# Four K tiles of a projection's last two column blocks as seven products, spread among plain chunks

## The chip, the cores and the metric

One NeuronCore of one Trainium2 chip runs the whole program. The metric is device time in microseconds (us) from the start to the end of one execution. A core has TensorE (PE; its weight loads are PEld), VectorE (DVE), ScalarE (ACT), GpSimd (POOL) and SyncE (SP); SP, and partly POOL and ACT, issue the DMA transfers. Each engine works through its own instructions in order, and semaphores hold one until another's result is there.

## The reference

A trunk of two encoder layers on x, 256 positions by 2048 channels in float32: an attention and pooling mixer, a gated MLP (FFN), an mLSTM mixer, and a second FFN. The change lies in the last step of the mLSTM mixer:

```python
hn = hsum * lax.rsqrt(jnp.mean(hsum * hsum, axis=-1, keepdims=True) + NORM_EPS)
hn = hn * h_norm.astype(jnp.float32).reshape(MLSTM_HEADS, MLSTM_HEAD_DIM)
y = (hn.reshape(b, s, MLSTM_W) * o_gate).astype(h.dtype)
return y @ w_out
```

`y` is 256x2048, `w_out` 2048x2048, and the product is added to x. x then goes through an RMS norm into the second FFN.

## The kernel before

**Precision and chunks.** Each operand of a matrix product is kept as a high and a low part in a format that TensorE takes at full rate, and a product is three matmuls (high x high, high x low, low x high). Weights stream from DRAM as chunks of 128x1024 (512 KB). `Stream.load` issues the transfer of a chunk into a raw buffer `w` (seven of them) on SP's queue, and `Stream.split` makes its two parts in `hl` (five buffers): ScalarE's cast for the high part (L167), VectorE's subtraction for the low one (L168). TensorE's instructions stand in the order in which the Python code writes them. In this layer the other engines' are ordered by a scheduler, which works with a model of its own of how long things take, at build time; on the chip each engine then keeps that order.

**The output projection.** `out_proj` multiplies the mixer's result `mcat` (16 K tiles of 128 channels, each with both parts, in two tiles of eight) by `w_out` in four column blocks of 512. A chunk holds two K tiles of one column block, that is 12 matmuls of 128x512 (2 K tiles, 2 row halves, 3 terms). Blocks 0 and 1 are built side by side, first the K tiles 0 to 11, then 12 to 15, which are the last two heads and come late. Then follow block 2 and block 3, eight chunks each. A block has a PSUM tile of two banks, of which there are two (`mm`). `residual` (L543) adds a finished block to x, and `norm.add` squares it and sends it through transposes (`xt`, L347) into the normed, transposed and split activation `xx` of the layer after (ScalarE's high half at L359, VectorE's low half at L362). One `xt` holds two K tiles in one bank.

**The small PSUM banks.** `psp` has two pools of two banks each. The transposes take them by turns; a tile can also ask for a side.

**The work woven in.** `Weave` runs generators while the projection's matmuls are recorded: the last two heads' gates (`og`, reciprocals at L997, `hn` at L1001), their transposes (`htr`, L1006), and the norm blocks.

**Preparation for the layer after.** The FFN's products already use sums of weight quarters. Some are made ahead, under this layer: a step loads 1 MB into `gm` (L120), VectorE makes four sums there in place (L124 to L127), and SP stores them to DRAM (L129). There is one `gm`, so the next load waits for the store. Where these steps stand is set by numbers of chunks (`places`). Others are made by transfers that add, issued by POOL (L139, L143). An FFN also has one more raw buffer, in memory that this layer gives back.

**Seven products.** The last FFN's down projection has a helper for two row halves and two column blocks at once. With A and B cut in quarters, `into` forms the result from seven products instead of eight. It takes a pair of K tiles at a time, four sums of quarters of A (`pair_sums`: six sums on VectorE, a cast, a low half) and four sums of quarters of B (`Stream.sums`: kind "sum" needs one 128x512 addition before its split, "chain" two, "left" one). It accumulates in four small banks, b1 and b5 on side 1, b6 and b4 on side 0, and adds them to x with plus and minus in nine 128x512 VectorE additions; one product is kept by a ScalarE copy (`ca`). A chunk of such a unit feeds two products, six matmuls.

Of the kernel before, what the change touches and what calls it, by code (L numbers as in the profile page):

```python
# [9 lines left out]
F32 = mybir.dt.float32  # L10
F32R = mybir.dt.float32r
# [5 lines left out]
P = 128  # L17
D = 2048
S = 256
KT = D // P  # L20
# [12 lines left out]
FCH = [4, 8, 8, 8, 8, 8]  # L33
DORDER = (0, 1, 3, 2)
# [3 lines left out]
WARM = 5  # L38
ATT_PARTS = [[4 + h for h in range(8)], [0, 1, 2, 3], [4 + h for h in range(8, 12)]]
ML_PARTS = [list(range(12)), list(range(12, 16))]  # L40

NG = 4 * KT
NB = D // 512
# [22 lines left out]
class Stream:  # L66
# [182 lines left out]
def trunk(ctx: ExitStack, tc: tile.TileContext, gx, xT, xn, call, catt, cml, weights, make, out):  # L249
    nc = tc.nc  # L250
    v, a, g, pe = nc.vector, nc.scalar, nc.gpsimd, nc.tensor

    def pool(name, bufs, **kw):
        return ctx.enter_context(tc.tile_pool(name=name, bufs=bufs, **kw))
# [9 lines left out]
    mmp = pool("mm", 2, space=PSUM)  # L264
# [22 lines left out]
    wv = Weave()  # L287
# [7 lines left out]
    def mm(out_, lhsT, rhs, start, stop):  # L295
        pe.matmul(out_, lhsT, rhs, start=start, stop=stop, skip_group_check=True)  # L296
# [211 lines left out]
    def mov_group(act, name, width=512, before=None, after=None):  # L508

        ps = mmp.tile([P, 2, 512 if width > 256 else width], F32, tag="mm", name=name)  # L510
        per = CH * P // width
        hl = None
        for k in range(KT):
            if k % per == 0:
                before and before(k)
                hl = st.next()
                after and after(k)
            src = act(k)
            c = (k % per) * width
# [20 lines left out]
    def residual(ps, b, eng=None):  # L540
        for t in range(2):
            xs = x[:, t, b * 512 : b * 512 + 512]
            v.tensor_add(xs, xs, ps[:, t])  # L543

    def out_proj(cat, norm, name, parts, ready):

        pss = [mmp.tile([P, 2, 512], F32, tag="mm", name=f"op{name}_{i}") for i in range(2)]
        for i, kts in enumerate(parts):
            ready(i)
            for ps in pss:  # L550
                mov_part(ps, cat, kts, i == 0, i == len(parts) - 1)
        for b in range(NB):
            if b >= 2:
                ps = mmp.tile([P, 2, 512], F32, tag="mm", name=f"op{name}_{b}")
                mov_part(ps, cat, sum(parts, []), True, True)
            else:
                ps = pss[b]
            residual(ps, b)
            norm.add(b)


    def attention_layer(norm, nxt):
        with ExitStack() as es:
            def lp(name, bufs):
                return es.enter_context(tc.tile_pool(name=name, bufs=bufs, reuse_waits="tile"))

            kp, tp, t1p = lp("att_c", 1), lp("att_t", 2), lp("att_1", 1)
            catb = []
# [154 lines left out]
            vt = kp.tile([P, 2, 2, 512], F32R, tag="vt", name="vt")  # L723
# [76 lines left out]
            ps = mov_group(xx, "kproj", 512, ahead, tables)  # L800
# [27 lines left out]
            def ready(i):  # L828
                wv.until(lambda: need[i] <= done)

            out_proj(cat, nxt, "0", ATT_PARTS, ready)


    def mlstm_layer(norm, nxt):
        with ExitStack() as es:
# [181 lines left out]
            for hp in range(MH // 2):  # L1017
                vf = t1p.tile([P, 2, 512], F32, tag="vf", name=f"mvf{hp}")
                for c, n in ((0, MD + 32), (MD, MD)) if hp == 0 else ((0, 512),):
                    ps = mov_group(xx, f"mv{hp}_{c}", n)  # L1020
# [19 lines left out]
            def ready(i):  # L1040
                wv.until(lambda: set(range(6 + 2 * i)) <= done)

            out_proj(cat, nxt, "1", ML_PARTS, ready)


    def ffn_layer(layer, norm, nxt):
# [259 lines left out]
def _mov(w):  # L1306

    return w.reshape(-1, 2, P, 512).transpose(0, 2, 1, 3).reshape(-1, P, CH * P)


def _out_chunks(w, parts):
    t = w.reshape(KT, P, D)

    def some(kts, c):
        return _mov(t[kts][:, :, c : c + 512].reshape(len(kts) * P, 512))

    out = [some(kts, c) for kts in parts for c in (0, 512)]
    return np.concatenate(out + [some(sum(parts, []), c) for c in range(1024, D, 512)])


def _half_chunks(t):

    t = t.reshape(-1, 2, P, 2, 512).transpose(0, 1, 3, 2, 4)[list(DORDER)]
    b11, b12, b21, b22 = (t[:, k, n] for k in range(2) for n in range(2))
    return (np.concatenate([b11, b12, b22, b21], axis=2), np.concatenate([b21[0::2], b21[1::2]], axis=2))


def _att_chunks(w_in, w_out):
    pool_w, q_w = 512, HEADS * HD
    cols = [pool_w + q_w, pool_w, pool_w + q_w + 512, pool_w + 512, pool_w + 1024]  # L1330
    a = [_mov(w_in[:, c : c + 512]) for c in cols]
    a += [_stat(w_in[:, c : c + 256], range(KT)) for c in (0, 256)]
    return np.concatenate(a), _out_chunks(w_out, ATT_PARTS)


def _ml_chunks(w_in, w_out):
    a = []
    for hp in range(MH // 2):
        c = 2 * D + hp * 512
        a.append(_mov(w_in[:, c : c + 512]) if hp else _stat(w_in[:, c + MD : c + 512], range(KT)))  # L1340
        for h in (2 * hp, 2 * hp + 1):
            for part in (0, 1):
                c = part * D + h * MD
                a.append(_stat(w_in[:, c : c + 256], range(KT)))
        wo = w_in[:, 3 * D + hp * 512 : 3 * D + hp * 512 + 512]
        a.append(_mov(wo))
    return np.concatenate(a), _out_chunks(w_out, ML_PARTS)


def _up_chunks(w):  # L1350
# [241 lines left out]
```

## Time and profile before

| what | us |
|---|---|
| median of 3 runs | 2149.03 |
| the profiled execution, its own time | 2149.48 |
| its span, first to last instruction | 2147.7 |
| TensorE busy in the span | 2141.4 |
| VectorE busy | 1808.7 |
| ScalarE busy | 1342.4 |

The profile is of one execution. Its span is 1.8 us shorter than its time, which includes what lies around the instructions. Busy time of TensorE counts pipelined matmuls, so that a matmul of 128x512 shows 390 ns though the next starts sooner. The projection of the mLSTM layer begins at 1353 us in the span and ends at 1446.

### The profile page before, as it was taken

Reading aid. Unit: us, or ns where it says so; the run is one execution under the profiler, and the core shown is the slowest. Engines: PE = TensorE matmul, PEld = TensorE weight load, DVE = VectorE, ACT = ScalarE, POOL = GpSimd, SP = SyncE. Lnnn points to the kernel's source line nnn. Section 1 sums busy time; section 2 is a strip of 40 time slices with the busy share of each in tenths; the row PEclk is TensorE's granted clock in tenths of the full one; section 3 lists DMA queues with packets and bytes.
Section 4 is the critical chain, followed back from the end, with each engine's and each line's share of the span. In section 5 each row is a group of like instructions: output and inputs, shape, how many; then the busy total and the mean of one; then the engine's idle time right before and its main releaser. Section 6 shows DMA issues by size and latency. Waiting matters only on the chain.

```text
span 2147.7 us, 31090 instructions
## 1 busy us (share of the span) xinstructions
PE 2141.4 (100%) x10740; PEld 1811.7 (84%) x10740; DVE 1808.7 (84%) x2553; ACT 1342.4 (63%) x1883; POOL 256.6 (12%) x320
## 2 busy tenths in 40 slices
PE   9999999999999999999999999999999999999999
PEld 7888888888888888889888888888888888888887
DVE  7686698989889798877888887779898888988998
ACT  7665566766567576656445554456675776766865
POOL 0222111111111111100000011101111111101000
PEclk9999999999999999999999999999999999999999
DMA  9989899999999999968898899988999999999985
GB/s 356 241 239 253 256 250 357 305 338 329 301 329 313 333 319 365 322 181 272 348 340 330 334 304 331 311 292 243 337 322 325 337 316 339 351 333 341 332 283 167
DMA packets 217520, 659.08 MB, mean 307 GB/s; under 512 B 27178, under 2 KB 29522, under 8 KB 210578
## 3 DMA queue, kind: packets, MB, share of 16 engines
q1 hardware_dynamic: 183280, 598.02, 76.8%
q0 software_dynamic: 31008, 55.33, 16.6%
q10 hardware_dynamic: 3074, 3.75, 0.7%
q8 instruction: 84, 1.38, 0.2%
q14 instruction: 74, 0.61, 0.1%
HBM read 627.58 MB, written 139.50 MB: 357 GB/s over the span
## 4 chain that ended last, share of the span: by engine, by line
PE 96%; DVE 2%; DMA 1%; issue 1%; ACT 0%; ACTq 0%; DVEq 0%; SPq 0%
PE dn L296 21%; PE p L296 21%; PE up L296 20%; PE op L296 6%; PE mk L296 4%; PE mq L296 4%; PE mo L296 4%; PE mv L296 4%; PE qproj L296 3%; PE kproj L296 1%; PE pool L296 1%; PE vproj L296 1%; PE tr L1183 1%; DVE hl L168 1%; PE h_dn L296 1%
## 5 line engine op out<-in xcount | busy, mean ns | idle before, releaser
L167 ACT CAST hl<-w 128x1024 fp32r<-128x1024 f32 (+2 forms) x921 | 954.3, 1048 | 584.4 <-PE dn L296 95.2
L168 DVE TENSOR_TENSOR hl<-w,hl 128x1024 fp32r<-128x1024 f32 (+1 forms) x922 | 1110.2, 1218 | 247.6 <-ACT hl L167 239.5
L296 PE MATMUL dn<-hl,g 128*128 128x512 f32 x1968 | 470.0, 391 | 0.0
L296 PE MATMUL up<-xx,hl 128*128 128x512 f32 (+1 forms) x2560 | 466.5, 337 | 0.0
L296 PEld LDWEIGHTS up<-xx,hl 128*128 128x128 f32 x2560 | 405.0, 188 | 63.7
L296 PEld LDWEIGHTS dn<-hl,g 128*128 128x128 f32 x1968 | 367.3, 188 | 75.4
L296 PE MATMUL p<-hl,sx 128*128 128x512 f32 x1152 | 304.2, 390 | 0.2 <-DVE hl L168 0.2
L296 PEld LDWEIGHTS p<-hl,sx 128*128 128x128 f32 x1152 | 212.2, 188 | 42.1 <-DVE hl L168 0.6
L296 PE MATMUL p<-hl,xx 128*128 128x512 f32 x864 | 236.3, 391 | 0.0
L139 POOL DMA_DIRECT2D G<-in_q x140 | 116.5, 838 | 653.0 <-DMA G<-in_q 625.3
L296 PEld LDWEIGHTS p<-hl,xx 128*128 128x128 f32 x864 | 158.2, 188 | 30.1
L143 POOL DMA_DIRECT2D G<-G x124 | 108.3, 874 | 555.9 <-DMA G<-in_q 218.6
L296 PE MATMUL mv<-hl,xx 128*128 128x512 f32 (+2 forms) x480 | 92.4, 350 | 0.0
L296 PE MATMUL mq<-xx,hl 128*128 128x512 f32 (+1 forms) x512 | 91.9, 337 | 0.0
L296 PE MATMUL mk<-xx,hl 128*128 128x512 f32 (+1 forms) x512 | 91.8, 338 | 0.0
L296 PE MATMUL op<-hl,cat 128*128 128x512 f32 x384 | 91.6, 393 | 0.0
L296 PE MATMUL mo<-hl,xx 128*128 128x512 f32 x384 | 90.4, 391 | 0.0
L296 PE MATMUL op<-hl,mcat 128*128 128x512 f32 x384 | 90.0, 392 | 0.3 <-DVE x L543 0.3
L296 PEld LDWEIGHTS mq<-xx,hl 128*128 128x128 f32 x512 | 79.2, 188 | 11.6
L296 PEld LDWEIGHTS mk<-xx,hl 128*128 128x128 f32 x512 | 78.8, 188 | 11.4
L296 PEld LDWEIGHTS mv<-hl,xx 128*128 128x128 f32 x480 | 78.1, 189 | 11.1
L296 PEld LDWEIGHTS op<-hl,mcat 128*128 128x128 f32 x384 | 71.3, 188 | 15.3 <-issue 0.7
(274 smaller groups left out, 2006.1 us busy)
## 6 DMA issues: line engine op xcount, KB each, us to landing
w<-in_dn SPq DMA_DIRECT2D x168, 512.0 KB, 7.6
w<-in_up SPq DMA_DIRECT2D x160, 512.0 KB, 8.0
w<-in_m_in SPq DMA_DIRECT2D x124, 512.0 KB, 6.4
w<-G SPq DMA_DIRECT2D x88, 512.0 KB, 8.4
w<-in_q SPq DMA_DIRECT2D x80, 512.0 KB, 8.5
G<-in_q SPq DMA_DIRECT2D x124, 256.0 KB, 7.7
G<-G POOLq DMA_DIRECT2D x124, 256.0 KB, 7.6
w<-in_q SPq DMA_DIRECT2D x120, 256.0 KB, 7.2
```

What stands on the lines that cost most here:

```text
L139: pin(add.dma_start(G[r, 0:512], src[r, 512:1024], accum_op=ALU.add))
L143: pin(add.dma_start(G[:, at : at + 512], G[:, of : of + 512], accum_op=ALU.add))
L167: (self.nc.vector.tensor_copy if i + c == 0 else self.nc.scalar.copy)(hl[:, 0, c : c + n], w[:, c : c + n])
L168: self.nc.vector.tensor_sub(hl[:, 1, c : c + n], w[:, c : c + n], hl[:, 0, c : c + n].bitcast(F32))
L296: pe.matmul(out_, lhsT, rhs, start=start, stop=stop, skip_group_check=True)
L1183: pe.transpose(tr[:, j, t * P : t * P + P], src[:, c : c + P], ident)
```

## The change

Blocks 0 and 1 stay as they were. In blocks 2 and 3 the K tiles 0 to 3 no longer go in plain chunks. They are one unit of seven products over both blocks: two pairs of K tiles, 7 chunks. Blocks 2 and 3 keep 6 plain chunks each, so the projection has 35 chunks where it had 32. After two plain chunks of block 2 the unit's chunks alternate with plain ones (four of block 2, two of block 3). The sums of A are made once the last heads are done (`cat_sums`), in tiles that the heads used; the kept product is `cam`. The weights are reordered on the host, outside the timed program. The numbers in `places` are moved by the three new chunks.

```diff
+ATT_HALF, ML_HALF = [], [0, 1, 2, 3]
...
+    def out_proj(cat, norm, name, parts, ready, tiles, half=None):
...
-        for b in range(NB):
-            if b >= 2:
-                ps = mmp.tile([P, 2, 512], F32, tag="mm", name=f"op{name}_{b}")
-                mov_part(ps, cat, sum(parts, []), True, True)
-            else:
-                ps = pss[b]
-            residual(ps, b)
+        for b in range(2):
+            residual(pss[b], b)
             norm.add(b)
+        rest = [k for k in sum(parts, []) if k not in tiles]
+
+        def block(b):
+            ps = mmp.tile([P, 2, 512], F32, tag="mm", name=f"op{name}_{b}")
+            for k in range(0, len(rest), 2):
+                last = k == len(rest) - 2
+                mov_part(ps, cat, rest[k : k + 2], k == 0, last)
+                if last:
+                    residual(ps, b)
+                yield
+
+        third, fourth = block(2), block(3)
+        if tiles:
+            next(third), next(third)
+            two, sum_of, room, sums_done = half
+            wv.until(lambda: norm.blocks == 2 and sums_done())
+            order = [(p, i) for p in range(len(tiles) // 2) for i in range(2)]
+            unit = into(2, two, sum_of, len(tiles) // 2, f"op{name}", order, room)
+            for _ in range(len(rest) // 2 - 2):
+                next(unit), next(third)
+            for _ in range(2):
+                next(unit), next(fourth)
+            next(unit)
+        for _ in third:
+            pass
+        norm.add(2)
+        for _ in fourth:
+            pass
+        norm.add(3)
...
+            def cat_sums():
+                sx.append(t1p.tile([P, 4, 2, 2, P], F32R, tag="vt", name="sxm"))
+                for p in range(2):
+                    tv = t1p.tile([P, 2, S], F32, tag="G", name=f"cs1{p}")
+                    raw = t1p.tile([P, 4, P], F32, tag="Amat", name=f"cr1{p}")
+                    pair_sums(two(p), tv, raw, [(slice(0, 4), sx[0][:, :, p, 0], sx[0][:, :, p, 1])])
+                    yield 3.5
+                sx.append(None)
...
-    at = len(weights) + len(ml)
+    at = len(weights) + len(ml) - 3
...
-    here = [(at + 8 + 14 * k, 5) for k in range(16)]
+    here = [(at + 11 + 14 * k, 5) for k in range(16)]
```

**Where instructions move.** VectorE ahead of the seventh head's last product `hn6`, whose transposes TensorE takes inside the projection. Before (`hl` are low halves of splits, `rv` and `re` the head's norm, `og` the gate, `gm` the prepared sums):

```order
L168 TENSOR_TENSOR hl538_12674<-w538_12598,hl538_12674 128x1024
L168 TENSOR_TENSOR hl539_12727<-w539_12619,hl539_12727 128x1024
L301 TENSOR_SCALAR rv_h7_12700<-hss7_12696 128x2
L168 TENSOR_TENSOR hl540_12745<-w540_12647,hl540_12745 128x1024
L305 TENSOR_TENSOR re_h7_12704<-ry_h7_12702 128x2
L306 TENSOR_TENSOR re_h7_12704<-re_h7_12704,rv_h7_12700 128x2
L307 TENSOR_SCALAR re_h7_12704<-re_h7_12704 128x2
L308 TENSOR_TENSOR re_h7_12704<-re_h7_12704,ry_h7_12702 128x2
L997 RECIPROCAL og6_12658<-og6_12658 128x256
L124 TENSOR_TENSOR gm_9031<-gm_9031 128x512
L168 TENSOR_TENSOR hl541_12762<-w541_12669,hl541_12762 128x1024
L1001 TENSOR_TENSOR hn6_12447<-hn6_12447,og6_12658 128x512
```

And now (`cs` and `cr` are the pair sums, `sxm` their low half):

```order
L169 TENSOR_TENSOR hl541_12762<-w541_12669,hl541_12762 128x1024
L451 SCALAR_TENSOR_TENSOR cr11_12981<-cr11_12981,cs11_12980 128x128
L452 TENSOR_TENSOR cr11_12981<-cr11_12981,cs11_12980 128x128
L307 TENSOR_TENSOR re_h7_12704<-re_h7_12704,rv_h7_12700 128x2
L453 TENSOR_TENSOR cr11_12981<-cr11_12981,cs11_12980 128x128
L308 TENSOR_SCALAR re_h7_12704<-re_h7_12704 128x2
L309 TENSOR_TENSOR re_h7_12704<-re_h7_12704,ry_h7_12702 128x2
L1022 RECIPROCAL og6_12658<-og6_12658 128x256
L125 TENSOR_TENSOR gm_9031<-gm_9031 128x512
L169 TENSOR_TENSOR hl542_12779<-w542_12718,hl542_12779 128x1024
L456 TENSOR_TENSOR sxm_12945<-cr11_12981,sxm_12945 128x4x128
L1026 TENSOR_TENSOR hn6_12447<-hn6_12447,og6_12658 128x512
```

Between the gate's reciprocals and `hn6` the pair sums have come in, and one split more (`hl542`). Ten rows of pair sums stand further ahead in the same stretch and are not shown.

TensorE at the start of block 2, before (`op1_2` is block 2, `xt3` the transposes of norm blocks 0 and 1):

```order
L347 MATMUL xt3_0_13055<-cst_87,x_90 128x128 x4
L296 MATMUL op1_2_13018<-hl551_12971,mcat0_10166 128x512 x6
L347 MATMUL xt3_2_13070<-cst_87,x_90 128x128 x4
L296 MATMUL op1_2_13018<-hl552_12991,mcat0_10166 128x512 x6
L347 MATMUL xt3_4_13090<-cst_87,x_90 128x128 x4
L296 MATMUL op1_2_13018<-hl552_12991,mcat0_10166 128x512 x6
L347 MATMUL xt3_6_13105<-cst_87,x_90 128x128 x4
L296 MATMUL op1_2_13018<-hl553_13029,mcat0_10166 128x512 x12
L296 MATMUL op1_2_13018<-hl554_13046,mcat1_11908 128x512 x12
```

And now (`h1`, `h5`, `h6`, `h4` are the unit's banks b1, b5, b6, b4):

```order
L348 MATMUL xt3_0_13079<-cst_87,x_90 128x128 x4
L297 MATMUL op1_2_13040<-hl551_12992,mcat0_10166 128x512 x6
L348 MATMUL xt3_2_13094<-cst_87,x_90 128x128 x4
L348 MATMUL xt3_4_13103<-cst_87,x_90 128x128 x4
L348 MATMUL xt3_6_13112<-cst_87,x_90 128x128 x4
L297 MATMUL h1_op1_13127<-hl552_13013,mcat0_10166 128x512 x3
L297 MATMUL h5_op1_13128<-hl552_13013,sxm_12945 128x512 x3
L297 MATMUL op1_2_13040<-hl553_13051,mcat1_11908 128x512 x12
L297 MATMUL h6_op1_13164<-hl554_13070,sxm_12945 128x512 x3
L297 MATMUL h4_op1_13165<-hl554_13070,mcat0_10166 128x512 x3
L297 MATMUL op1_2_13040<-hl555_13123,mcat1_11908 128x512 x12
```

The last two transposes follow the second directly, and right behind the fourth the unit starts, which takes all four small banks.

VectorE at the same place, before (`xx` from `xt3_6` are the low halves of K tiles 6 and 7):

```order
L168 TENSOR_TENSOR hl556_13117<-w556_13019,hl556_13117 128x1024
L362 SCALAR_TENSOR_TENSOR xx3_9018<-xt3_2_13070,gcol_88,xx3_9018 128x256
L362 SCALAR_TENSOR_TENSOR xx3_9018<-xt3_4_13090,gcol_88,xx3_9018 128x256
L362 SCALAR_TENSOR_TENSOR xx3_9018<-xt3_2_13070,gcol_88,xx3_9018 128x256
L124 TENSOR_TENSOR gm_9031<-gm_9031 128x512
L362 SCALAR_TENSOR_TENSOR xx3_9018<-xt3_4_13090,gcol_88,xx3_9018 128x256
L125 TENSOR_TENSOR gm_9031<-gm_9031 128x512
L168 TENSOR_TENSOR hl557_13138<-w557_13044,hl557_13138 128x1024
L362 SCALAR_TENSOR_TENSOR xx3_9018<-xt3_6_13105,gcol_88,xx3_9018 128x256
L126 TENSOR_TENSOR gm_9031<-gm_9031 128x512
L168 TENSOR_TENSOR hl558_13155<-w558_13079,hl558_13155 128x1024
```

And now:

```order
L169 TENSOR_TENSOR hl556_13138<-w556_13041,hl556_13138 128x1024
L363 SCALAR_TENSOR_TENSOR xx3_9018<-xt3_6_13112,gcol_88,xx3_9018 128x256
L363 SCALAR_TENSOR_TENSOR xx3_9018<-xt3_0_13079,gcol_88,xx3_9018 128x256
L363 SCALAR_TENSOR_TENSOR xx3_9018<-xt3_2_13094,gcol_88,xx3_9018 128x256
L363 SCALAR_TENSOR_TENSOR xx3_9018<-xt3_4_13103,gcol_88,xx3_9018 128x256
L125 TENSOR_TENSOR gm_9031<-gm_9031 128x512
L363 SCALAR_TENSOR_TENSOR xx3_9018<-xt3_6_13112,gcol_88,xx3_9018 128x256
L126 TENSOR_TENSOR gm_9031<-gm_9031 128x512
L127 TENSOR_TENSOR gm_9031<-gm_9031 128x512
L128 TENSOR_TENSOR gm_9031<-gm_9031 128x512
L169 TENSOR_TENSOR hl557_13159<-w557_13068,hl557_13159 128x1024
```

The low halves and the four sums of `gm` have moved ahead of the split `hl557`, which before stood behind the second sum. The second low half from `xt3_6` stands behind the first sum of `gm` in both.

More of the change, by code (lines that the diff above doesn't have):

```diff
@@ L543, in residual @@
             v.tensor_add(xs, xs, ps[:, t])
-    def out_proj(cat, norm, name, parts, ready):
+    def out_proj(cat, norm, name, parts, ready, tiles, half=None):
         pss = [mmp.tile([P, 2, 512], F32, tag="mm", name=f"op{name}_{i}") for i in range(2)]
@@ L829, in ready @@
                 wv.until(lambda: need[i] <= done)
-            out_proj(cat, nxt, "0", ATT_PARTS, ready)
+            out_proj(cat, nxt, "0", ATT_PARTS, ready, ATT_HALF)
     def mlstm_layer(norm, nxt):
@@ L1041, in ready, with two, ready_sums @@
                 wv.until(lambda: set(range(6 + 2 * i)) <= done)
-            out_proj(cat, nxt, "1", ML_PARTS, ready)
+            sx = []
+            def two(p):
+                return catb[0][:, 2 * p : 2 * p + 2]
+            def cat_sums():
[6 more added lines that the diff above has]
+                sx.append(None)
+            def ready_sums(i):
+                ready(i)
+                if i == 1:
+                    wv.add(cat_sums())
+            half = (two, lambda j, p: [sx[0][:, j, p, i, :] for i in range(2)],
+                    lambda: t1p.tile([P, 512], F32, tag="og", name="cam"), lambda: len(sx) > 1)
+            out_proj(cat, nxt, "1", ML_PARTS, ready_sums, ML_HALF, half)
     def ffn_layer(layer, norm, nxt):
@@ L1308, in _mov, with _out_chunks @@
     return w.reshape(-1, 2, P, 512).transpose(0, 2, 1, 3).reshape(-1, P, CH * P)
-def _out_chunks(w, parts):
+def _out_chunks(w, parts, tiles):
     t = w.reshape(KT, P, D)
@@ L1317, in _out_chunks, with _out_order, _half_chunks @@
     out = [some(kts, c) for kts in parts for c in (0, 512)]
-    return np.concatenate(out + [some(sum(parts, []), c) for c in range(1024, D, 512)])
-def _half_chunks(t):
-    t = t.reshape(-1, 2, P, 2, 512).transpose(0, 1, 3, 2, 4)[list(DORDER)]
+    rest = [k for k in sum(parts, []) if k not in tiles]
+    out = {"out": np.concatenate(out + [some(rest, c) for c in range(1024, D, 512)])}
+    if tiles:
+        w = t[tiles][:, :, 1024:].reshape(len(tiles) * P, 1024)
+        out["four"], out["last"] = _half_chunks(w, range(len(tiles) // 2))
+    return out
+def _out_order(out, four=(), last=()):
+    if not four:
+        return out
+    n = (len(out) - KT) // 2
+    third, fourth = out[KT : KT + n], out[KT + n :]
+    unit = [(kind, q[:, c : c + 1024]) for q in four for kind, c in (("sum", 0), ("chain", 1024))]
+    unit += last + [("left", q[:, 512:1536]) for q in four]
+    plain = third[2:] + fourth[:2] + [None]
+    both = [e for pair in zip(unit, plain, strict=True) for e in pair]
+    return out[:KT] + third[:2] + both[:-1] + fourth[2:]
+def _half_chunks(t, order):
+    t = t.reshape(-1, 2, P, 2, 512).transpose(0, 1, 3, 2, 4)[list(order)]
     b11, b12, b21, b22 = (t[:, k, n] for k in range(2) for n in range(2))
@@ L1332, in _att_chunks @@
     a += [_stat(w_in[:, c : c + 256], range(KT)) for c in (0, 256)]
-    return np.concatenate(a), _out_chunks(w_out, ATT_PARTS)
+    return np.concatenate(a), _out_chunks(w_out, ATT_PARTS, ATT_HALF)
 def _ml_chunks(w_in, w_out):
@@ L1346, in _ml_chunks @@
         a.append(_mov(wo))
-    return np.concatenate(a), _out_chunks(w_out, ML_PARTS)
+    return np.concatenate(a), _out_chunks(w_out, ML_PARTS, ML_HALF)
 def _up_chunks(w):
@@ L1545 @@
         "call": call, "catt": catt, "cml": cml, "m_g": m_g,
-        "a_in": a_in, "a_out": a_out, "m_in": m_in, "m_out": m_out,
+        "a_in": a_in, "m_in": m_in, **{f"a_{k}": e for k, e in a_out.items()}, **{f"m_{k}": e for k, e in m_out.items()},
     }
@@ L1551 @@
         if HALF[l]:
-            arrays[f"hq{l}"], arrays[f"hb{l}"] = _half_chunks(i["w_down"][l][sum(FCH[:-1]) * P :, :1024])
+            arrays[f"hq{l}"], arrays[f"hb{l}"] = _half_chunks(i["w_down"][l][sum(FCH[:-1]) * P :, :1024], DORDER)
         arrays[f"q{l}"], arrays[f"b{l}"] = _quad_chunks(i["w_up"][l], UNITS[l])
@@ L1569 @@
     pairs = [_pairs(l, t[f"q{l}"]) for l in range(2)]
-    att, ml = chunks("a_in") + chunks("a_out"), vg + chunks("m_in") + chunks("m_out")
+    a_out, m_out = (_out_order(**{k: chunks(f"{n}_{k}") for k in e}) for n, e in (("a", a_out), ("m", m_out)))
+    att, ml = chunks("a_in") + a_out, vg + chunks("m_in") + m_out
     weights = att + ffn(0)
@@ L1581 @@
     pairs[1] += [(f"1h_{p}", 1, t["hq1"][p]) for p in range(4)]
-    places[1] += [(at + 246 + 14 * k, 6) for k in range(4)]
+    places[1] += [(at + 249 + 14 * k, 6) for k in range(4)]
     make = {}
```

## The prediction

> **What bounds the kernel now.** I read the page first, then TensorE's waits, then the stages of the projection, then its instructions engine by engine. The page's busy part and the largest groups, TensorE's waits, and four stages of the projection (busy us and instruction count for PE, PEld, DVE, ACT, POOL, then clock, DMA share, GB/s):
>
> ```profile
> span 2147.7 us, 31090 instructions
> PE 2141.4 (100%) x10740; PEld 1811.7 (84%) x10740; DVE 1808.7 (84%) x2553; ACT 1342.4 (63%) x1883; POOL 256.6 (12%) x320
> PE 96%; DVE 2%; DMA 1%; issue 1%; ACT 0%; ACTq 0%; DVEq 0%; SPq 0%
> ...
> L296 PE MATMUL op<-hl,mcat 128*128 128x512 f32 x384 | 90.0, 392 | 0.3 <-DVE x L543 0.3
> ```
>
> ```profile
> PE wps L320 <- DVE pad L762: 1.2, 1, 1.2
> PE htr L1006 <- DVE hn L1001: 0.3, 1, 0.3
> PE op L296 <- DVE x L543: 0.3, 1, 0.3
> ```
>
> ```profile
> 1353.00:1375.00 22.00, 22.00 (x106) 18.39 (x105) 20.13 (x26) 11.49 (x18) 3.15 (x4) 1.00 0.94 284
> 1375.00:1400.00 25.00, 24.70 (x111) 20.18 (x110) 13.99 (x18) 9.76 (x13) 2.44 (x3) 1.00 0.97 314
> 1400.00:1420.00 20.00, 20.00 (x97) 16.51 (x97) 13.88 (x20) 12.28 (x22) 2.59 (x4) 1.00 1.00 349
> 1420.00:1446.00 26.00, 26.00 (x120) 21.51 (x119) 16.42 (x19) 13.75 (x19) 1.52 (x2) 1.00 0.78 250
> ```
>
> TensorE is the chain, and its longest wait after the start is 0.3 us. So every matmul removed is a gain in full, and every wait added is a loss in full. Behind it VectorE has 64.4 of 93 us in the projection, 91% of the first stage. What decides the change is where VectorE and the transfers stand in order, not their sums.
>
> **The matmuls removed.** TensorE's part of the chain (start, us, what):
>
> ```profile
> 1399.76 4.37 PE op L296 x18
> ...
> 1409.62 0.44 PE xt L347 x4
> 1410.05 17.74 PE op L296 x78
> 1427.79 0.44 PE xt L347 x4
> ```
>
> 78 matmuls in 17.74 us: 0.227 us each, a plain chunk of 12 is 2.73 us, a unit's chunk of 6 is 1.36. Four K tiles in two column blocks are 48 matmuls; 2 pairs x 7 products x 3 are 42. Six fewer: **-1.4 us**.
>
> **Work added at nothing, if only totals counted.** Three chunks more (1.57 MB, 4.5 us at 349 GB/s, under the last stage's 22% of idle transfer time); three casts, two of the sums and one copy on ScalarE, some 5 us beside 47 busy of 93. VectorE gets three splits, eight weight additions, two pair-sum sets and nine additions into x and the kept product: about 18 us at the durations below, beside 64 busy of 93. The moved preparation numbers (+11, +249) keep their distance to the layer after. If the totals were the whole story the answer would be -1.4.
>
> **First place: the head's transpose.** VectorE in order (start, us, idle before it), and the transpose on TensorE:
>
> ```profile
> 1328.95 0.69 DVE L534 TENSOR_TENSOR tb_k<-mk,tb_k 128x512 f32<-128x512 f32 x1 [0.31 <-ACT tb_k L533]
> ...
> 1341.34 0.69 DVE L124 TENSOR_TENSOR gm<-gm 128x512 f32<-128x512 f32 x1 [1.04 <-DMA gm<-in_q]
> ...
> 1351.41 1.23 DVE L168 TENSOR_TENSOR hl<-w,hl 128x1024 fp32r<-128x1024 f32 x1 [1.41 <-ACT hl L167]
> ...
> 1354.82 0.77 DVE L995 TENSOR_SCALAR og<-og 128x512 f32<-128x512 f32 x2 [1.38 <-ACT og L991]
> ...
> 1361.52 1.23 DVE L168 TENSOR_TENSOR hl<-w,hl 128x1024 fp32r<-128x1024 f32 x1 [0.39 <-ACT hl L167]
> ...
> 1366.67 0.69 DVE L1001 TENSOR_TENSOR hn<-hn,og 128x512 f32<-128x512 f32 x1
> ...
> 1372.49 0.63 DVE L127 TENSOR_TENSOR gm<-gm 128x512 f32<-128x512 f32 x1
> ```
>
> ```profile
> 1369.76 0.60 PE L1006 MATMUL htr<-cst,hn 128*128 128x128 f32 x4
> ```
>
> hn ends at 1367.4 and is wanted at 1369.8: 2.4 us of slack. Ahead of it now stand ten 128x128 sums, a 128x512 sum, two low halves, one split and one sum of gm. The pair sums of the last layer price them, and splits and additions follow each other closer than their durations, as the x3 and the x2 show (a 128x128 sum by the same measure some 0.21):
>
> ```profile
> L448 DVE TENSOR_TENSOR cr<-cs x4: 283/288/293, 2041.4 to 2116.2; 128x128 f32<-128x128 f32 x4
> L455 DVE TENSOR_TENSOR sx<-cr,sx x4: 683/686/692, 2054.9 to 2121.8; 128x512 fp32r<-128x512 f32 x4
> ```
>
> ```profile
> 1420.89 3.49 DVE L168 TENSOR_TENSOR hl<-w,hl 128x1024 fp32r<-128x1024 f32 x3
> 1424.29 1.28 DVE L543 TENSOR_TENSOR x<-x,op 128x512 f32<-128x512 f32 x2
> ```
>
> That is 10 x 0.21 + 4 x 0.60 + 1.14 = 5.6 us. The gm set of 1341.34, for which VectorE waits 1.0 already, comes 1.6 us late as well: among the sums whose store it follows now stand the pair's first sum and tb_k, two of 0.6, with the 0.31 of wait. The three idle stretches shown absorb at most 3.2. hn is late by 5.6 + 1.6 - 3.2 = 4.0, less 2.4 of slack: **+1.6 us** (bounds: 0 if the idle stretches of other rows absorb it, 2.5 if only two of the three do). The last sum of that gm set then ends near 1378.0, not 1373.1: hn at 1371.3 and behind it 6.7 us of rows (three sums, hn of the second head, two splits, a reciprocal of 1.64, an mcat of 0.4).
>
> **Second place: the start of block 2.** VectorE and the two gm sets behind it:
>
> ```profile
> 1392.39 0.69 DVE L124 TENSOR_TENSOR gm<-gm 128x512 f32<-128x512 f32 x1 [5.92 <-DMA gm<-in_q]
> ...
> 1396.59 0.69 DVE L127 TENSOR_TENSOR gm<-gm 128x512 f32<-128x512 f32 x1
> ...
> 1398.34 1.28 DVE L543 TENSOR_TENSOR x<-x,op 128x512 f32<-128x512 f32 x2
> ...
> 1410.11 0.87 DVE L362 SCALAR_TENSOR_TENSOR xx<-xt,gcol,xx 128x256 fp32r<-128x256 f32 x2
> ...
> 1415.03 0.69 DVE L124 TENSOR_TENSOR gm<-gm 128x512 f32<-128x512 f32 x1 [3.41 <-DMA gm<-in_q]
> ```
>
> ```profile
> 1394.11 1.05 ACT L167 CAST hl<-w 128x1024 fp32r<-128x1024 f32 x1 [1.67 <-PE op L296]
> ```
>
> A gm set waits for the store of the last (L129) and a load (L120); each took, from issue to landing (min/median/max):
>
> ```profile
> DMA to landing us min/median/max: 5.6/8.1/11.2
> ```
>
> ```profile
> DMA to landing us min/median/max: 5.4/8.3/10.3
> ```
>
> From the end of one set to the next is so 16.4 us by the medians; the two above took 19.3 (from 1373.1) and 17.8 (from 1397.3). Taking 16.4 (the queues are no fuller than there), the set comes at 1378.0 + 16.4 = 1394.4, two sums, a split whose cast (the row on ScalarE) waits for TensorE and so ends 1.6 later, at 1396.8, a weight sum, a sum and the two additions: x is done at 1400.3. Blocks 0 and 1 end on TensorE at 1399.76 - 0.3, and 1.6 later now: 1401.1. So the 0.3 us wait there goes: **-0.3**. With 19.3 it is 0.9 of wait instead.
>
> **Third place: the unit's first chunk.** This is the term that decides. Its products take four PSUM banks at once (side 1 for b1 and b5), and the four transposes of norm blocks 0 and 1 have just filled the same four. b1 needs the bank of K tiles 2 and 3, b5 that of tiles 6 and 7, so both wait until VectorE has read the last low half from it. Before, nobody wanted these banks until the next transposes, at 1427.79. In the new order VectorE reaches tile 7's low half after the first sum of the next gm set, and that waits for its load.
>
> TensorE would be at b5 at 1401.1 + 2 x 2.73 + 4 x 0.44 + 0.68 = 1409.0. VectorE: the gm set ends at 1400.9, plus 16.4 is 1417.3, one sum 0.60, one low half 0.48: 1418.4. Wait: **+9.4 us**, in two pieces around the three products of b1.
>
> Bounds: even with the gm load there at once, VectorE has 17.8 us of rows from 1394.4 to that low half (five gm sums, six splits, four weight sums, four additions, eight low halves at 0.4) and stops for ScalarE's casts, which stand behind squares: 1414.8 at the earliest, a wait of 5.8. With the two durations seen it is 1421.3, against TensorE at 1410.0: 11.3, and 0.9 at the start of block 2.
>
> After that the splits of the next four chunks are done, and TensorE needs 8.9 us for them; the split behind (L168) ends 3 us after the release. No further wait of weight until the FFN by this count.
>
> **Sum**: -1.4 + 1.6 - 0.3 + 9.4 = +9.3, on the profiled execution's own 2149.48: 2158.8. The median of the runs, 2149.03, stands 0.45 lower, so **2158.4 us**. Its own range by the bounds of the third place (an earlier or later hn only shifts time between the waits): -1.4 + 1.6 - 0.3 + 5.8 = +5.7 and -1.4 + 1.6 + 0.6 + 11.3 = +12.1, that is 2155 to 2161.
>
> **Rivals.**
> *The gain arrives alone.* If ScalarE and VectorE clear both banks by 1407.4, no wait starts and hn is in time: -1.4 - 0.3, 2147.3 us. For it: VectorE is idle for 28.6 of those 93 us. Against it: the row of 5.92 us, an engine stopped by its order with work behind it. It decides at 1409.0 for tile 7's low half; my earliest is 1414.8.
>
> *The clock falls after the wait.* The warm-up at the program's start and the same shape late:
>
> ```profile
> L320 PE MATMUL wps<-x x10: 379/634/792, 1.2 to 4.9; 128*128 128x256 f32 x10
> ```
>
> ```profile
> L296 PE MATMUL npr<-dg,cst x4: 379/380/381, 265.9 to 1456.4; 128*128 128x256 f32 x4
> ```
>
> ```profile
> 1456.38 0.43 PE npr L296 x2
> ```
>
> The same matmul took up to 792 ns just after launch and 380 in the stream, though the clock column says 1.00 there. If 9 us of idle brings that back, the first ten or so matmuls behind it run at half speed: the ten took some 4.1 us (1.2 to 4.9 and one of 0.4), at the spacing of the others (0.43 a pair, in the chain) 2.15, so 1.9 us: 2160.3. For it: the waits of 6 and 3 us have no like in the trace; against it: three products lie between, and only the launch shows it. [...]
>
> *The layer after loses its start.* One load for the FFN was issued 70 us early; now it is among the last, since its room is freed by the unit's last product.
>
> ```profile
> 1376.73 0.66 SPq L101 DMA_DIRECT2D w<-in_up x1
> ```
>
> Its split stands ahead of block 3's addition on VectorE, and the transposes of tiles 12 and 13 wait for that addition. It lands some 8 us (as the loads above) after the projection's last split frees the queue; at worst 2.5 us on TensorE: 2160.9.
>
> **Chances.** The forecast's waits alone 0.45; with the clock 0.27; with the FFN's start or both 0.13; the gain alone, or next to it, 0.15. The range reaches down into the last and up over both others: 2150.5 to 2164.5. A measurement of this kernel tells about 2%, 43 us, from no change. No case comes near it: same 0.99, faster 0, slower 0.01.
>
> **What would show it.** A row of TensorE h_op with several us of idle, released by VectorE xx, near 1409; a wait of htr for hn near 1370; VectorE's stop at gm between tile 7's two low halves; the op group at 336, h_op at 42. The prediction is wrong if TensorE's waits in the projection sum to under 3 us, if the wait falls on a split or a weight load instead of xx, or if the loss is after the projection's last matmul.

## The result, and the profile after

| | runs | median us | range us | ratio to before (95%) |
|---|---|---|---|---|
| before | 6 | 2149.20 | 2148.96 to 2149.34, and one of 2351.26 | |
| after | 6 | 2164.91 | 2162.16 to 2166.16 | 1.0071 (1.0060 to 1.0082) |

The one run of 2351.26 us is a slow one and stands outside the ratio. The change costs 15.7 us, 0.7%. The forecast was 2158.4, +9.3; the median lies 0.4 us above the upper end of the range. By the bound of 2% it is no change, as given.

The profiled execution took 2166.16 us, at the upper end of the six, with a span of 2164.4. First its busy part and the chain by engine, from the page:

```profile
span 2164.4 us, 31131 instructions
...
PE 2144.5 (99%) x10734; PEld 1812.9 (84%) x10734; DVE 1825.7 (84%) x2587; ACT 1347.1 (62%) x1889; POOL 257.6 (12%) x320
...
PE 91%; DMA 4%; DVE 3%; issue 1%; ACT 0%; SPq 0%; ACTq 0%; DVEq 0%
```

TensorE has six matmuls fewer (10734 for 10740), and its "busy" is even 3 us higher, since slow matmuls count. The chain, which ran through TensorE for 96%, now leaves it for DMA and VectorE. TensorE's waits:

```profile
PE h_op L297 <- DVE xx L363: 6.6, 2, 5.8
PE p L297 <- DVE hl L169: 2.5, 1, 2.5
PE op L297 <- DVE x L544: 1.7, 1, 1.7
PE atr L990 <- DVE A L982: 1.6, 1, 1.6
PE htr L1031 <- DVE hn L1026: 1.5, 2, 1.2
...
PE p L297 <- ACT tb L1231: 1.0, 1, 1.0
```

Here h_op are the unit's products, op those of the plain chunks, and p those of an FFN unit; atr and htr are transposes, of a head's own tile A (not the A whose quarters are summed) and of hn. Before, none after the start was over 0.3. The two of p are in the FFN, near 1843 us and later; the others are in and just ahead of the projection, but for 0.3 of htr, which stood there before too. TensorE in order of time (start, us, what, idle before it):

```profile
1404.32 4.37 PE L297 MATMUL op<-hl,mcat 128*128 128x512 f32 x18 [1.69 <-DVE x L544]
...
1410.35 1.47 PE L348 MATMUL xt<-cst,x 128*128 128x128 f32 x12
1417.65 1.62 PE L297 MATMUL h_op<-hl,mcat 128*128 128x512 f32 x3 [5.83 <-DVE xx L363]
1420.08 1.62 PE L297 MATMUL h_op<-hl,sxm 128*128 128x512 f32 x3 [0.81 <-DVE xx L363]
1421.50 4.56 PE L297 MATMUL op<-hl,mcat 128*128 128x512 f32 x12
1425.89 0.86 PE L297 MATMUL h_op<-hl,sxm 128*128 128x512 f32 x3
...
1459.72 3.64 PE L297 MATMUL up<-xx,hl 128*128 128x512 f32 x20
```

The unit's first two products wait for the banks of the transposes, in two pieces, as forecast. Behind them the same kind of products take 1.62 us for three where 0.86 is usual, and a chunk of twelve takes 4.56 for 2.9. The stages show why: the granted clock (the first number behind POOL's) falls to half.

```profile
1410.00:1415.00 5.00, 1.82 (x15) 1.46 (x13) 3.97 (x6) 4.02 (x8) 0.00 (x0) 0.98 1.01 390
1415.00:1420.00 5.00, 1.62 (x3) 0.83 (x3) 4.05 (x9) 2.01 (x6) 0.79 (x1) 0.50 1.00 348
1420.00:1425.00 5.00, 4.92 (x12) 3.89 (x13) 4.07 (x6) 1.04 (x1) 0.85 (x1) 0.50 0.58 211
```

What VectorE did meanwhile:

```profile
1344.94 0.69 DVE L125 TENSOR_TENSOR gm<-gm 128x512 f32<-128x512 f32 x1 [4.69 <-DMA gm<-in_q]
...
1399.22 0.69 DVE L125 TENSOR_TENSOR gm<-gm 128x512 f32<-128x512 f32 x1 [5.08 <-DMA gm<-in_q]
...
1418.85 0.69 DVE L125 TENSOR_TENSOR gm<-gm 128x512 f32<-128x512 f32 x1 [0.95 <-DMA gm<-in_q]
1419.46 0.48 DVE L363 SCALAR_TENSOR_TENSOR xx<-xt,gcol,xx 128x256 fp32r<-128x256 f32 x1
```

The first row is a stop just ahead of the projection, of which more below. The other two are at the last two gm sets, and the low half that frees the second bank is the instruction behind the second stop: it begins at 1419.46 and TensorE starts at 1420.08. In the chain of waits these transfers now stand for a third each of the time from 1375 to 1425:

```profile
1380.23 9.37 DMA G<-gm
1389.62 9.58 DMA gm<-in_q
...
1404.80 7.04 DMA G<-gm
...
1411.91 6.92 DMA gm<-in_q
```

Before, VectorE read that bank just as late:

```profile
1420.49 0.48 DVE L362 SCALAR_TENSOR_TENSOR xx<-xt,gcol,xx 128x256 fp32r<-128x256 f32 x1
```

It cost nothing, as nobody wanted the bank until 1427.79. The change has not made VectorE's work late; it has made somebody wait for it.

**Where the time went.** The FFN's first product began at 1446.26 before (in the trace's list of instructions) and at 1459.72 now: +13.46. From there to the end of the span it was 2147.7 - 1446.26 = 701.4 and is 2164.4 - 1459.72 = 704.7: +3.2. Up to the FFN the starts of consecutive matmuls give: six matmuls fewer -1.4, atr +1.7, hn +1.4, x +1.4, the banks +6.8, the slower clock +3.3 (spacings of 0.43 for 0.227), the rest +0.3.

### The profile page after: what moved, and what is told of

It is laid out like the page before. It is cut to its first block, busy times and chain, and to the rows that moved or that the text cites. A ratio compares the mean times of both kernels' runs of the same rounds, so it can differ in the third digit from the quotient of the medians.

```text
span 2164.4 us, 31131 instructions
## 1 busy us (share of the span) xinstructions
PE 2144.5 (99%) x10734; PEld 1812.9 (84%) x10734; DVE 1825.7 (84%) x2587; ACT 1347.1 (62%) x1889; POOL 257.6 (12%) x320
## 4 chain that ended last, share of the span: by engine, by line
PE 91%; DMA 4%; DVE 3%; issue 1%; ACT 0%; SPq 0%; ACTq 0%; DVEq 0%
PE p L297 21%; PE up L297 20%; PE dn L297 20%; PE op L297 6%; PE mk L297 3%; PE mo L297 3%; PE mq L297 3%; PE qproj L297 3%; PE mv L297 3%; DMA G<-gm 2%; DMA gm<-in_q 2%; DVE hl L169 1%; PE kproj L297 1%; PE pool L297 1%; PE vproj L297 1%; PE tr L1229 1%
## 5 line engine op out<-in xcount | busy, mean ns | idle before, releaser
L297 PEld LDWEIGHTS mo<-hl,xx 128*128 128x128 f32 x384 | 71.0, 188 | 14.1
L297 PE MATMUL op<-hl,mcat 128*128 128x512 f32 x336 | 81.1, 398 | 1.7 <-DVE x L544 1.7
```

## The experiments

| run | us median (n) | ratio to before (95%) | FFN's first product | half-speed stretch, us |
|---|---|---|---|---|
| the change | 2164.91 (6) | 1.0071 (1.0060 to 1.0082) | 1459.72 | 10.2 |
| e1_no_gm | 2158.83 (5) | 1.0044 (1.0031 to 1.0057) | 1452.29 | 6.8 |
| e2_fill | 2161.15 (5) | 1.0059 (1.0046 to 1.0072) | 1458.64 | 3.4 |
| e3_no_sums | 2163.99 (5) | 1.0067 (1.0053 to 1.0081) | 1455.24 | 10.2 |
| e4_norm_late | 2160.34 (5) | 1.0046 (1.0033 to 1.0059) | 1452.33 | 0 |
| e5_ffn_turns | 2161.28 (5) | 1.0054 (1.0041 to 1.0066) | 1458.14 | 10.2 |
| e6_before_ffn_turns | 2154.34 (11) | 1.0023 (1.0014 to 1.0032) | 1447.42 | 0 |
| e7_late_norm_and_sums | 2155.70 (8) | 1.0028 (1.0018 to 1.0039) | 1452.15 | 3.4 |
| e8_late_unit | 2162.85 (5) | 1.0062 (1.0048 to 1.0076) | 1455.87 | 10.2 |
| e9_gm_behind_splits | 2151.13 (11) | 1.0009 (1.0000 to 1.0018) | 1447.93 | 0 |
| e10_two_gm_later | 2150.27 (11) | 1.0003 (0.9994 to 1.0012) | 1444.87 | 0 |
| e11_two_gm_between | 2149.88 (11) | 1.0002 (0.9993 to 1.0011) | 1446.87 | 0 |

Medians of before beside them: 2149.15 to 2149.68. The last two columns are of the profiled execution, the last one only up to the FFN.

### e1: without the last two sets of gm

```diff
+SKIP = {"151_6", "151_7"}
...
-        if kind == 4:
+        if kind == 4 and key in self.skip:
+            if part == 0:
+                pin(sync.dma_start(G, src))
+        elif kind == 4:
```

> Left out: the four sums of the last two prepared sets (gm), of which one stands ahead of x in block 0 and one between tile 7's two low halves; their data goes from DRAM to DRAM unsummed, so the last unit of the FFN computes with wrong weights. Theory (VectorE stands at gm, and the load into the one gm buffer decides when the unit's banks come free): the 5.1 us stop at 1394 and the 1.0 us stop at 1418 go, and with them the casts that came late because SP's queue stood at gm's store; the wait for x (1.7) goes and the waits of h_op fall from 6.6 to under 3.5, so the idle stretch is short enough for the clock to stay 1.00: 2164.9 - 1.7 - 3.1 to 6.6 - 2.4 = 2154 to 2158. Rival (the banks come free by the transposes, high and low halves alone, gm or not): the waits of h_op stay above 5 us, the clock still falls, 2162 to 2165.

2158.83, 6.1 us less than the change, just above the theory's 2158. VectorE's stops at these two sets are gone, and the wait for x with them. (The 1.6 us of atr are absent too, though the orders of VectorE and SP ahead of it are those of the change; more on this wait below.) One wait for the banks is left, and the half-speed stretch is 6.8 us, shorter but not gone as the theory had it:

```profile
PE h_op L301 <- DVE xx L367: 3.5, 1, 3.5
PE p L301 <- DVE hl L173: 2.5, 1, 2.5
PE htr L1035 <- DVE hn L1030: 1.5, 2, 1.2
```

So gm, its sums and its transfers together, accounts for 3.1 of the 6.6 us at the banks (VectorE is done with them 7.6 us earlier, and TensorE is there 3.7 us earlier). The rest is there without it: the last transposes end at 1408.13, and VectorE still has three splits, a weight sum and the eight low halves from 1404.28 to 1412.31.

### e2: work for TensorE during the wait

```diff
+            free = mmp.tile([P, 2, 512], F32, tag="mm", name=f"op{name}_3")
...
+            for _ in range(26):
+                mm(free[:, 0], cat(0)[:, 0, 0:P], cat(0).rearrange('p a b -> p (a b)'), True, True)
             unit = into(2, two, sum_of, len(tiles) // 2, f"op{name}", order, room)
```

> Added: 26 matmuls of 128x256 columns and more, with a result that nobody reads, between the transposes and the unit's first product, into the bank that block 3 takes later; TensorE stays busy where it waited, for some 3 us by half-width matmuls at 0.11 us each. Theory (the first part of the 15.7 us is a wait whose end VectorE sets, the second a clock that falls to half after the idle stretch): the end of the wait does not move, h_op still waits, but for 3 us less; if the idle stretch that remains is too short to lower the clock, the granted clock stays 1.00 and the 2.4 us of slow matmuls behind the release go: 2161 to 2163. Rival (the slow matmuls come from something else, such as the small banks or the sums of A as operands): the clock still shows 0.5 near 1420, or h_op's first three matmuls still take 1.6 us, and the time is 2164 to 2168.

The expectation has the fill's size wrong: these matmuls are 128x512, 26 of them 6.1 us. They replaced the first piece of the wait fully, and the end of the second stayed where it was (1419.72 for 1420.08). VectorE's and SP's instructions have the order of the change from first to last, so the wait's end is VectorE's, as the theory says:

```profile
1410.28 6.17 PE L297 MATMUL op<-mcat 128*128 128x512 f32 x26
1416.40 0.93 PE L297 MATMUL h_op<-hl,mcat 128*128 128x512 f32 x3
1419.72 1.11 PE L297 MATMUL h_op<-hl,sxm 128*128 128x512 f32 x3 [2.38 <-DVE xx L363]
1420.63 4.36 PE L297 MATMUL op<-hl,mcat 128*128 128x512 f32 x12
```

The median is 3.8 us lower with work that nobody needs. That it is a gain isn't clear of noise: the runs overlap (2160.39 to 2165.11 here, 2162.16 to 2166.16 in the change), and the two profiled executions differ by 1.05. The theory's clock of 1.00 did not come. In the profiled execution it fell after only 2.4 us of idle, but for a third of the time (0.66 in one stage of 5 us). In the other four the mean granted clock is 0.998 or 0.999, where every run of before beside them has 1.000, so it fell somewhere in them too. The profiled execution is the longest of the five; why the others are shorter was not seen.

### e3: without the sums of A

```diff
-                if i == 1:
-                    wv.add(cat_sums())
...
+            half = (two, lambda j, p: [two(p)[:, j // 2, i, j % 2 * P : j % 2 * P + P] for i in range(2)],
+                    lambda: t1p.tile([P, 512], F32, tag="og", name="cam"), lambda: True)
```

> Left out: the sums of quarters of A (two sets of pair sums on VectorE, their casts on ScalarE); the products take plain quarters in their place, so the output is wrong. Theory (the sums come ahead of A, hn and a gm set on VectorE, and all that follows is late by their time): the waits of atr (1.6) and htr (1.2) go, the gm set before 1380 ends 5 to 6 us earlier and each later one as well, and tile 7's last low half comes near 1414 instead of 1419.9. The unit then waits 5 to 6 us at most from an arrival at 1407.7, and the clock still falls: 2157 to 2161. Rival (the early waits only take time out of the late one, since gm's loads run by their own durations): the end of the last low half stays within 1.5 us, 2163 to 2166.

2163.99: by the time the rival's range, by the trace the theory. The waits of atr, of htr in the projection and for x are gone, and the bank is free at 1416.07, 4.0 us earlier. TensorE was there earlier too, so its idle stretch is a single one of 9.32 us. In this execution the clock also fell at the FFN's wait of 2.5 us: the eleven matmuls of p behind it (1841.38 to 1845.45) took 4.07 us where the change's take 2.64, and the mean granted clock is 0.997, where 10.2 us at half speed alone would leave 0.998. From the FFN's first product to the end it took 706.3 us, 1.6 more than in the change. So the FFN begins 4.5 us earlier and the median is 0.9 lower; that the clock fell at the FFN in the other four executions as well would fit, but only one is profiled. Their mean granted clocks say as much: 0.997 in three of the four, as in the profiled one, where the change's profiled execution has 0.998 with its 10.2 us.

### e4: the norm's transposes behind the unit

```diff
         for b in range(2):
             residual(pss[b], b)
-            norm.add(b)
+            if not tiles:
+                norm.add(b)
...
-            wv.until(lambda: norm.blocks == 2 and sums_done())
+            wv.until(sums_done)
...
+        if tiles:
+            norm.add(0), norm.add(1)
         norm.add(2)
```

> Moved: the squares and transposes of norm blocks 0 and 1 stand behind the unit's last product, so the unit finds the four small banks free. gm, the sums of A and the weight sums stay. Theory (the unit waits for its banks, and only for them): both waits of h_op go (6.6) and the clock stays at 1.00 (2.4), the waits of atr, htr and x stay (4.5): 2164.9 - 9.0 = 2156, 2153 to 2159, unless the start of the FFN now waits for the six transposes behind the unit, which takes some of it back. Rival (VectorE and the weight stream are late anyway, so the unit's products wait for splits in place of banks): waits of h_op on hl of over 4 us, 2161 to 2165.

2160.34. The waits for banks are gone, the unit's products are not slowed (0.84 to 0.86 us for three, where none waits for a split), and the first of them follows the plain chunk at once, at 1409.18. TensorE's waits:

```profile
PE atr L993 <- DVE A L985: 2.5, 1, 2.5
PE p L297 <- DVE hl L169: 2.5, 1, 2.5
PE htr L1034 <- DVE hn L1029: 1.5, 2, 1.2
...
PE up L297 <- DVE xx L363: 1.1, 1, 1.1
PE p L297 <- ACT tb L1234: 1.0, 1, 1.0
PE h_op L297 <- DVE hl L169: 0.8, 1, 0.8
PE xt L348 <- DVE xx L363: 0.4, 1, 0.4
```

It lies 1.3 us above the range. In the profiled execution, the longest of the five (they start at 2155.77), three things took time back. The start of the FFN took 1.5, the named exception. The wait of atr came out 0.9 longer, with the same order of VectorE's and SP's instructions up to there. And behind the FFN's wait of 2.5 us the clock fell (0.999 in the mean): eleven matmuls of p took 4.22 us where the change's take 2.64, 1.6 us more.

### e5 and e6: the FFN's buffer turns

The FFN's chunks take an extra raw buffer every eighth time and an extra split buffer every sixth, by their number in the whole program. Three chunks more in the projection move these turns, and the scheduler (the planner of the expectations) then finds another order for VectorE's, ScalarE's and SP's instructions in the FFN. e5 undoes that in the changed kernel (shift 3), e6 does it alone in the kernel before (shift -3):

```diff
-        return ((self.wpool if i % 8 < 7 else self.more[0]) if raw else
-                (self.spool if i % 6 < 5 else self.more[1]))
+        return ((self.wpool if (i - self.shift) % 8 < 7 else self.more[0]) if raw else
+                (self.spool if (i - self.shift) % 6 < 5 else self.more[1]))
...
+            st.shift = 3 * layer      # e5; in e6 -3 * layer
```

> The changed kernel with one thing undone: in the last FFN, the chunk that takes the extra raw buffer (each eighth) and the extra split buffer (each sixth) is counted from three chunks later, so each of the FFN's chunks has the home that it had before the change; the order of every engine in the FFN is then that of the kernel before. Theory (the three added chunks move the turns of the buffers, the planner puts the FFN's splits in another order, and that costs two waits, 2.5 and 1.0 us): both waits go, the stretch from the FFN's first product to the end is 701.4 us as before and not 704.7, and the time falls by 3 to 5 us, to 2160 to 2162. Rival (the late waits come from the sums that are prepared late, or from transfers that the projection delays): the waits stay, 2163 to 2166.

> The kernel before with that one thing done: the turns of the extra buffers in the last FFN moved by three chunks, no unit and no added chunk in the projection; the FFN's order is that of the changed kernel. Theory: the waits of 2.5 and 1.0 us appear without the change's products, 2149.2 + 3.3 = 2152.5, 2152 to 2154.5 (more where the 2.5 us of idle lower the clock). Rival: 2149 to 2150.

Both as the theory has it. e5: 2161.28, and from the FFN's first product to the end 2159.4 - 1458.14 = 701.3 us; in the trace VectorE's and ScalarE's instructions of the FFN have the order of before. e6: 2154.34, 5.0 slower than before without a single product changed, with the two waits of the changed kernel:

```profile
PE p L296 <- DVE hl L168: 2.5, 1, 2.5
PE wps L320 <- DVE pad L762: 1.2, 1, 1.2
PE p L296 <- ACT tb L1185: 1.0, 1, 1.0
PE op L296 <- DVE mcat L1011: 1.0, 2, 0.8
```

The fourth row is new: 1.0 us in the projection. There one of the FFN's loads now stands between the projection's in SP's queue (at 1390.54), and VectorE's mcat rows stand behind splits whose cast it waits for, up to 6.8 us. That puts the FFN's first product 1.2 us later, and the FFN's part is 2152.3 - 1447.42 = 704.9, +3.5.

### e7: three causes undone

As e5 and e4, and the sums of A pinned behind the last head's product (each sum and low half of `pair_sums` in program order).

> Three edits at once, as a version that could beat both: the FFN's buffer turns as before, the squares and transposes of norm blocks 0 and 1 behind the unit, and the sums of A held on VectorE behind the last head's product. Theory (wait for banks, early sums and buffer turns are all of it): waits of atr, htr and of the banks go, what stays is up to 5 us of waits for splits and at the start of the FFN; 2148 to 2153. If some cost is not among the three, 2155 or more.

2155.70, so something else was left. Its longest wait:

```profile
PE h_op L297 <- DVE hl L169: 4.2, 2, 4.0
```

VectorE there, in order of time:

```profile
1411.74 0.69 DVE L125 TENSOR_TENSOR gm<-gm 128x512 f32<-128x512 f32 x1 [5.29 <-DMA gm<-in_q]
1412.35 1.22 DVE L169 TENSOR_TENSOR hl<-w,hl 128x1024 fp32r<-128x1024 f32 x1
```

gm again: its sum now stands ahead of the split for the unit's second chunk (the second row), and VectorE waits 5.29 us for the load.

### e8: the unit 5.5 us later

As e5, the sums of A pinned, and the unit behind four plain chunks of block 2 where it was two; the norm stays ahead of it.

```diff
-            next(third), next(third)
+            for _ in range(4):
+                next(third)
...
-            for _ in range(len(rest) // 2 - 2):
+            for _ in range(len(rest) // 2 - 4):
                 next(unit), next(third)
-            for _ in range(2):
+            for _ in range(4):
                 next(unit), next(fourth)
```

> The FFN's buffer turns as before, the sums of A held behind the last head's product, and the unit two plain chunks (5.5 us) later, with the transposes of norm blocks 0 and 1 ahead of it, as in the change. Theory (the end of the wait is set by the place of gm's sums on VectorE and their load; tile 7's last low half stands behind three of these sums and two splits): VectorE reads that bank near 1420, TensorE would be there at 1413, so 5 to 7 us of wait and the slower clock stay: 2154 to 2159. Rival (time alone, 5.5 us later is enough for VectorE): waits of h_op under 1.5 us, 2148 to 2151.

The median, 2162.85, is above the range, and so is the profiled execution with 2160.82: the waits for the banks are 7.9 us where 5 to 7 were forecast, and the FFN's start waits 1.5 us more. The place is as the theory has it. Tile 7's last low half stands behind gm's sums and comes at 1422.03; TensorE waits 4.9 and 3.0 us:

```profile
1418.01 1.62 PE L297 MATMUL h_op<-hl,mcat 128*128 128x512 f32 x3 [4.90 <-DVE xx L363]
1422.66 1.62 PE L297 MATMUL h_op<-hl,sxm 128*128 128x512 f32 x3 [3.03 <-DVE xx L363]
```

5.5 us more of useful work ahead of the unit bought nothing (e5, which differs in this and in the pinned sums, has 2161.28), since this low half now stands behind all four of gm's sums, where in the change it stands behind the first.

### e9, e10, e11: gm out of the way

e9 is e7 with the last set's sums six chunks behind their load; e10 and e11 move the last two sets. Of the line that changes, only the end is shown:

```diff
-[(at - 60 + 7 * k, 1, 5) for k in range(8)]
+[(at - 60 + 7 * k, 1, 5) for k in range(7)] + [(at - 11, 6, 10)]                  # e9
+[(at - 60 + 7 * k, 1, 5) for k in range(6)] + [(at - 18, 6, 9), (at - 8, 5, 9)]   # e10
+[(at - 60 + 7 * k, 1, 5) for k in range(6)] + [(at - 18, 7, 9), (at - 8, 6, 10)]  # e11
```

> The version with three edits and one more: the sums of the last prepared set stand six chunks behind their load and no longer one, so that on VectorE they come behind three more splits (hl554, hl555, hl557 among them), and the load is there by then. Theory (the 5.3 us for which VectorE stood at this set at 1411.7 are the cause of the unit's wait of 4.0 us for a split and of the clock behind it): that wait goes, the clock stays 1.00, 2155.7 - 4.0 - 1.7 = 2150, 2148 to 2151.5. Rival (VectorE has too much work between x's first addition and the second chunk of the unit, gm or not): a wait for a split of over 2 us stays, 2153 to 2156.

> The version with four edits, and the last two prepared sets later: set 6's sums six chunks behind its load, set 7's load three chunks later and its sums five behind it. On VectorE all sums of A now come ahead of set 6, in the 4 us for which VectorE stood at that set before. Theory (what is left of the loss, 3 us up to the FFN, is VectorE's work between 1410 and 1447, where it is busy nearly throughout): some 2 us of it come earlier, the two waits for splits of 0.7 us go, 2148.5 to 2150.5. Rival (the sets of gm only stop VectorE elsewhere): a new wait of over 1 us at the chunks hl554 to hl563, 2151 to 2154.

> As the one before, with set 6's sums between those of A (seven chunks behind the load), and set 7's six behind its load. Theory: as there, 2148.5 to 2150.5; the stop at set 6 falls at 1396, when its load has long landed. Rival: VectorE stands at set 7 near hl560, and the unit's later chunks wait, 2151 to 2154.

e9 falls to 2151.13, in the theory's range: the wait of 4.0 is gone, the clock stays (1.000 in the mean), two waits for splits of 0.7 are left. In e10 the sums of A fill VectorE's former stop at 1388, and TensorE's waits after the start are as small as in the kernel before:

```profile
PE htr L1034 <- DVE hn L1029: 0.3, 1, 0.3
PE tr L1232 <- DVE c L1209: 0.2, 1, 0.2
PE p L297 <- DVE hl L169: 0.2, 1, 0.2
PE xt L348 <- DVE xx L363: 0.2, 1, 0.2
```

Its span is 2146.4 us. Its FFN begins at 1444.87, 1.39 us ahead of the kernel before: the six matmuls, 1.36, arrive in full. That execution took 2148.13, the fastest of eleven whose median is 2150.27; before has 2149.18 (21 runs, the lowest 2148.82). Two of the eleven, 2148.13 and 2148.29, lie below all of before's. e11, with one wait of 0.8 for a split left, has 2149.88. The medians of e10 and e11 lie in the range of their theories, and by the medians no version here beats the kernel before. Why the others of e10 are up to 3.4 us slower than its profiled one was not seen, as only one execution is profiled; it is not the clock, which is 1.000 in all eleven.

## Why the prediction was right in direction and short in size

- **The matmuls, -1.4**: right; e10 shows them as -1.39 when nothing is in the way.
- **First place, hn, +1.6**: 1.2 of wait, 1.4 with what lies around it. But the wait of atr, a little earlier, was not in the sum. It is not firm: 1.6 here, 0.9 in e2, 2.5 in e4, none in e1 and e5, with the same order of VectorE's instructions up to there. VectorE stood 4.69 us at a gm set ahead of it; between 1285 and 1350 it stood at gm for 12.8 us in the change and 14.4 in e4, the two with the longest waits, and for 5.2 in e2, 5.3 in e5 and 3.7 in e1. So the wait goes, roughly, with how long VectorE stands at gm in an execution; why that differs was not seen.
- **Second place, x, -0.3**: wrong, +1.4. The step that failed is the choice of 16.4 us for gm's store and load by the medians of all such transfers. The two cases quoted beside it, in the stretch itself, were 19.3 and 17.8; here it was 19.7, from the last sum's end at 1379.5 to 1399.22. The text gave "With 19.3 it is 0.9 of wait instead", and for this turn that was the end to take.
- **Third place, the banks, +9.4**: mechanism, engine, instruction and the two pieces right; 6.6 us of wait, since TensorE came there 3.5 us later than forecast (1410.35 + 1.47 + 0.68 = 1412.5 for 1409.0) through the waits ahead. What counts is when the bank comes free: 1418.4 forecast, 1420.08 measured, 1.7 us of the miss. That this is so near is in part luck: of the two turns of gm ahead of it, both taken as 16.4, the first took 19.7 and the second, from 1404.77 to 1418.85, only 14.1. As for the bounds, the lower one has 2.6 us of stops without rows, and the upper one comes to 1421.5 by its own terms, not 1421.3. e1, e2 and e4 show the three parts of the wait: gm, VectorE's time, the bank.
- **"No further wait of weight until the FFN by this count"**: no wait, but slow matmuls. The clock was a rival with 0.27 at +1.9; it came true, with 3.3. The size was short because it took the ten slow matmuls of the launch, 4.1 us of them, as the length; the half-speed stretch was 10.2 us, and 15 matmuls of the unit and of the chunk behind it, all of 128x512, fell into it. The three products between the two waits, which the text put against the rival, did not keep the clock up.
- **The FFN, nothing**: wrong, +3.2. The prediction looked at one load of the FFN and at totals ("keep their distance to the layer after"). That the three chunks shift the turns of two buffers, and so the scheduler's order of the whole FFN, was in no step and no rival; e5 and e6 show it from both sides. The rival that was there, a late start of the FFN, did not come true: its first products have no wait in the change, and the two waits come some 385 and 580 us later.

Together: 9.3 forecast, +1.7 for the bank, +2.4 of the clock behind the second product (the earlier part lies in the wait), +3.2 in the FFN is 16.6, of 16.7 in the span.

The rival "the gain arrives alone" is what e10's profile shows, in the fastest of its executions, once the banks, the sums, gm and the turns are each dealt with.

## What to carry to other kernels

A resource that is read late without harm is a debt: before another user is given it, look up when it is really read, and which stop on the reading engine stands ahead of that. Count waits by when the last one ends; earlier ones only eat into it, and idle on TensorE can cost again in clock, as 2.4 us of it did in e2. Where buffers go round by a running number, adding chunks in one place can reorder a later stage, as it did the FFN here, so compare the orders there too before costing it at nothing.

## What the runs showed of the hardware

The clock falls after shorter idle than the prediction took: 2.4 us in e2. In the FFN a wait of 2.5 us lowered it in the profiled executions of e3 and e4 (eleven matmuls of p behind it took 4.07 and 4.22 us), and not in those of the change (2.64, at a granted clock of 1.00), e1 (2.63), e6 (2.62) and e2 (0.999 in the mean, which its 3.4 us at half speed in the projection account for). (In nine of e6's eleven executions the mean granted clock is 0.999, so there it fell somewhere too.) The half-speed stretches in the projection were 3.4, 6.8 or 10.2 us, and did not go by the idle time:

| run | idle of TensorE there, us | half-speed stretch, us |
|---|---|---|
| e3 | 9.32 | 10.2 |
| the change | 5.83 and 0.81 | 10.2 |
| e5 | 5.87 and 1.59 | 10.2 |
| e8 | 4.90 and 3.03 | 10.2 |
| e7 | 3.98 | 3.4 |
| e1 | 3.55 | 6.8 |
| e2 | 2.38 | 3.4 |

In the change the waits of 1.6 us for A and 1.7 us for x left the clock at 1.00. What decides whether 2.5 us of idle lower the clock, and for how long, was not shown.
